# Half of the conditioning product moved from GpSimd and TensorE to row sums on VectorE

## The chip, the core and the metric

The kernel runs on one core of a Trainium2 chip. The core has a matrix engine (TensorE, PE in the profile; its loads of weights are shown as PEld), VectorE (DVE), ScalarE (ACT), GpSimd (POOL) and SyncE (SP), whose queue issues all the transfers of this kernel. Every engine runs its own queue in order, and engines wait for each other through semaphores. The metric is the device time of one execution in microseconds (us); lower is better.

## The reference

One decoder block over 1024 tokens of width 1024, float32. A conditioning vector `c` gives six vectors of 1024 that shift, scale and gate the two halves of the block:

```python
cond = jax.nn.silu(c)
mod = (cond @ w_ada[l] + b_ada[l]).astype(x.dtype)
sh_a, sc_a, gt_a, sh_m, sc_m, gt_m = [m[:, None, :] for m in jnp.split(mod, N_MOD, axis=-1)]

h = rms_norm(x, g_attn_pre[l]) * (1 + sc_a) + sh_a
proj = h @ w_in[l]
...
mixed = jnp.concatenate([rms_norm(oa, g_mix_a[l]), rms_norm(ob, g_mix_b[l])], axis=-1)
y = mixed @ w_out[l]
x = x + gt_a * rms_norm(y, g_attn_post[l])

h = rms_norm(x, g_mlp_pre[l]) * (1 + sc_m) + sh_m
y = jnp.square(jax.nn.relu(h @ w_up[l])) @ w_down[l]
x = x + gt_m * rms_norm(y, g_mlp_post[l])
```

`oa` and `ob` are the outputs of two attention mixers, a sliding window with sinks and a mixture of dilated windows. This study is about `sh_m` and `sc_m`, the shift and scale of the second modulation. They depend on `c` alone, and the first who needs them is the normalised input of the MLP.

## The kernel before

**Order of the work.** The program is written by a planner, the class `Sched` (lines 190 to 338). The kernel registers steps with an engine, a guessed duration, the steps they depend on and the buffers they take and give; `run` always emits the step that can start first by its own clock. What comes out is a fixed order for each engine. Buffers are counted in `Res` objects, such as `r_stg` for the ring of five staging tiles of 128x1024 (`stage`, line 471) and `r_wa` for the ring of first-modulation weights. So any edit of a duration, a buffer count or a step's start can reorder everything that the planner places after it.

**Stages.** In the start, until about 66 us, `x` is normalised and modulated, and the first of six projection units runs as its input comes in. The first modulation is made there on VectorE: `condb` (line 605) holds the vector `cond` spread over all 128 partitions; the host has laid out the first 2048 columns of `w_ada` by output channel (`w_mod`, line 117), a channel per partition, so that one multiply with a row sum (`ada_chunk`, line 687) gives 128 channels. `condb` lies in the pool `p0`, which is closed when the attention's pools open. Then units 1 to 5 of the projections (tile `pj`, lines 909 to 912) are interleaved on TensorE with the attention of the units already projected: scores (`s_ps`), softmax on VectorE, ScalarE and GpSimd (`p_sb`), transposes (`pt_ps`), the split of P into a high half on ScalarE and a low half on VectorE (`ph`, lines 1391 and 1495), and P times V (`o_ps`). The far branch of the dilated mixer has a chain of small VectorE steps (lines 1257 to 1291, tiles `z_far`, `y_far`, `a_far`) ahead of its scaling on GpSimd (line 1298). Projections end at about 356 us; the output projection (`y_ps`, lines 1815 to 1817) and the second normalisation follow, and from 473.7 us on the MLP (`mlp_ps`, lines 2250 to 2252) fills the rest.

**The rest of `mod`.** Columns 2048 to 6143 of `w_ada` are worked off in 32 pieces by `ada_piece` (line 1040), four pieces to a group of 512 columns. Groups 0 and 1 are the first gate, groups 2 and 3 `sh_m`, groups 4 and 5 `sc_m`, groups 6 and 7 the second gate. A piece loads 512 KB into a staging tile (`wa_st`, line 1046). Pieces 0 to 23 run on GpSimd: twice a product with a column of `cond` (line 1061; the first of a group writes the sum directly, line 1057) and an addition to `ada_acc` (line 1062). At a group's end TensorE sums `ada_acc` over the partitions. For a gate that is one matmul with a matrix of ones (line 1075); for shift and scale four matmuls of one column each turn the row into columns (line 1078), and VectorE adds the bias (lines 1109 to 1112). `feed_ada` (line 1115) lets piece i start when `st.d`, the count of projection units done, passes 1.0 + i * 4.1 / 24. Pieces 24 to 31 run on VectorE in the MLP (line 1059).

Of the kernel before, what the change touches and what calls it, by code (L numbers as in the profile page):

```python
# [10 lines left out]
F32 = mybir.dt.float32  # L11
# [4 lines left out]
ALU = mybir.AluOpType  # L16
# [3 lines left out]
P = 128  # L20
D = 1024
S = 1024
KC = D // P
# [54 lines left out]
def _columns():  # L78

    out = []  # L80
    for u in range(6):
        if u > 1:
            q = [512 + 128 * u + 64 * h for h in range(2)]
            k, v = [x + 512 for x in q], [x + 1024 for x in q]
            parts, rows = PARTS_B, ROWS_B
        else:
            g = u
            q, k, v = [256 * g + 64 * h for h in range(4)], [512 + 64 * g], [640 + 64 * g]
            parts, rows = PARTS_A, ROWS_A
        for c in range(3):  # L90
            got = [h + d for h in v for d in range(64)] if c == 2 else []
            got = [0] * (P - len(got)) + got
            for p, n, step, whose, row, ds in parts[c]:
                heads = q if whose == "q" else k
                got[p:p + n * step:step] = [h + rows[row + ds * r] for r in range(n // len(heads)) for h in heads]
            out += got
    return out


def _host(inputs):  # L100

    h = {n: np.ascontiguousarray(inputs[n]) for n in _INS if n != "w_mod"}
    c = np.zeros((P, CW), np.float32)
    c[:, CW_C:CW_C + KC] = inputs["c"][0].reshape(P, KC)
    c[:, CW_SINK:CW_SINK + 8] = inputs["sink_a"]
    b = inputs["b_ada"][0].reshape(48, P)
    c[:, CW_COL:CW_COL + 56] = np.concatenate(
        [inputs["g_attn_pre"][0].reshape(8, P), inputs["g_mlp_pre"][0].reshape(8, P), b[0:16], b[24:40],
         inputs["g_mix_a"][0].reshape(4, P), inputs["g_mix_b"][0].reshape(4, P)]).T
    w = h["w_in"][0][:, _columns()].reshape(2, 4, P, 18, P)  # L110
    w = np.ascontiguousarray(w.transpose(3, 0, 2, 1, 4)).reshape(36, P, 512)

    w[:6] = w[:6].reshape(3, 2, P, 4, P).transpose(2, 1, 3, 0, 4).reshape(P, 6, 512).transpose(1, 0, 2)
    h["w_in"] = w

    w = inputs["w_ada"][0][:, :2 * D].reshape(P, KC, 2, KC, P)
    h["w_mod"] = np.ascontiguousarray(w.transpose(3, 2, 4, 1, 0)).reshape(KC, 2, P, D)
    h["positions"] = np.ascontiguousarray(inputs["positions"][0].reshape(TB, P).T)
    _constants(c)
    h["consts"] = c  # L120
    return {n: h[n] for n in _INS + ["consts"]}


def _constants(c):
    c[:, CW_ID:CW_ID + P] = np.eye(P, dtype=np.float32)
    p = np.arange(P)[:, None]
    d = p + 384 - np.arange(512)[None, :]
    mult = ((d >= 0) & (d <= 128)).astype(int)
    mult += (d >= 0) & (d <= 512) & (d % 4 == 0)
    mult += (d >= 0) & (d % 16 == 0)  # L130
    neg = np.array([BIG, 0.0, -np.log(2.0), -np.log(3.0)], np.float32)
    c[:, CW_MB:CW_MB + 512] = neg[mult]
    d = p + P - np.arange(256)[None, :]
    c[:, CW_MN:CW_MN + P] = np.where(d <= 128, 0.0, BIG)[:, :P]
    c[:, CW_MN + P:CW_MN + 256] = c[:, CW_MB + 384:CW_MB + 512]
    c[:, CW_MF:CW_MF + P] = neg[(d <= 128).astype(int) + (d % 4 == 0)][:, :P]
    c[:, CW_MA:CW_MA + 256] = np.where((d >= 0) & (d <= 127), 0.0, BIG)
    m = np.arange(P)[None, :]
    c[:, CW_SW:CW_SW + P] = p % 32 == m // 4
    c[:, CW_SW + P:CW_SW + 2 * P] = p // 4 == m % 32  # L140
    c[:, CW_PK:CW_PK + 4] = p % 4 == m[:, :4]
    c[:, CW_PK + 4:CW_PK + 8] = p // 32 == m[:, :4]
    c[:, CW_SCL] = np.where(p[:, 0] % 2, 1.0, -0.125)
    c[:, CW_SCL + 1] = np.where(p[:, 0] < 64, -0.125, 1.0)
    c[:, CW_F:CW_F + 8] = np.array(INV_FREQ, np.float32)[None, :]
# [44 lines left out]
class Sched:  # L190
# [20 lines left out]
    def op(self, eng, dur, emit, deps=(), **kw):  # L211

        o = self.step(dur, emit, deps, **kw)
        o.alts = None
        if isinstance(eng, str):
            self.queue[eng].append(o)
        else:
            o.alts = dict(zip(eng, zip(dur, emit)))
            for e in eng:
                self.queue[e].append(o)  # L220
        return o.ev
# [131 lines left out]
def t_dv(n):  # L353
    return 0.066 + 0.00104 * n
# [19 lines left out]
def hybrid_block(ctx: ExitStack, tc: tile.TileContext, x, positions, w_mod, w_ada, b_ada, g_attn_post, w_in, w_out,  # L374
                 g_mlp_post, w_up, w_down, consts, out):
    nc = tc.nc
    ctx.enter_context(tc.manual_schedule())
    V, A, G, T = nc.vector, nc.scalar, nc.gpsimd, nc.tensor
    x, out = x[0], out[0]
    w_ada, w_out, w_up, w_down = w_ada[0], w_out[0], w_up[0], w_down[0]  # L380
    sc = Sched()
    op, pe_op = sc.op, sc.pe_op

    def pool(name, bufs=1, side="left", space=None, stack=ctx):
        kw = dict(name=name, bufs=bufs, reuse_waits="tile")
        if space is not None:
            kw["space"] = space
        else:
            kw["side"] = side
        return stack.enter_context(tc.tile_pool(**kw))  # L390
# [18 lines left out]
    r_pj, r_x, r_t, r_s, r_o, r_d = Res(2), Res(1), Res(2), Res(2), Res(1), Res(0)  # L409
    r_stg, r_w, r_wst, r_hl = Res(5), Res(WR), Res(WS), Res(0)  # L410
# [10 lines left out]
    cols = head[:, CW_COL - 8:CW_COL + 56]  # L421
# [6 lines left out]
    b1m = const.tile([P, KC], F32, name="b1m")  # L428
    g_a = const.tile([P, KC], F32, name="g_a")
    s_a = const.tile([P, KC], F32, name="s_a")  # L430
    g_m = const.tile([P, KC], F32, name="g_m")
    s_m = const.tile([P, KC], F32, name="s_m")
# [23 lines left out]
    p0 = pool("p0", 1, "right", stack=right0)  # L456
    pj = pool("pj", 2, space=PSUM)
    px = pool("px", 1, space=PSUM)
# [7 lines left out]
    st = Tok()  # L466
# [4 lines left out]
    def stage(name):  # L471
        return stgp.tile([P, 1024], F32, name=name, tag="stg")

    def load(emit, nbytes, deps=(), takes=(), prio=5, gives=(), after=None, n=1):
        return op("SP", nbytes / (345e3 if prio > -500 else 370e3), emit, deps, takes=takes, prio=prio, gives=gives, after=after, n=n)
# [16 lines left out]

    posi = p0.tile([P, TB], I32, name="posi")
    posf = p0.tile([P, TB], F32, name="posf")
    NWA, NH = 6, 3
    r_h = Res(NH)

    order0 = [("x", 0), ("x", 1), ("x", 2), ("x", 3), (0, 1), (0, 0), ("w", 0)]
# [99 lines left out]
    def f_cond():  # L598
# [3 lines left out]
        bc["diag"] = place0("diag")  # L602
        V.tensor_tensor(by_k(bc["diag"]), ident.unsqueeze(1).to_broadcast([P, KC, P]),
                        cond[:].unsqueeze(2).to_broadcast([P, KC, P]), ALU.mult)
    condb, bc = p0.tile([P, D], F32, name="condb"), {}
    e = e_cond = op("DVE", 0.52 + t_dv(D), f_cond, [e], takes=[(r_wa, 1)], prio=0)
    e_condb = []
    for n in range(2):
# [394 lines left out]
    def open_attention():  # L1003
        if any(x.t is None for x in e_tab[0] + e_tab[1] + list(e_hl.values())):
            return False
        nonlocal kring, qring, vfring, pprob, pth, opool, adp, mask_a, mask_b, mask_n, mask_f, swap, pick, e_mask
        right0.close()
        kw = dict(side="right", stack=right1)
        mkp = pool("mkp", 1, **kw)
        kring = pool("kring", NK, **kw)  # L1010
        qring = pool("qring", NQ, **kw)
        vfring = pool("vfring", NF, **kw)
        pprob = pool("pprob", NP, **kw)
        pth = pool("pth", NT, **kw)
        opool = pool("op", NO, **kw)
        adp = pool("adp", 1, **kw)
        r_k.give(sc.clk["PE"], NK)
        r_q.give(sc.clk["PE"], NQ)
        r_vf.give(sc.clk["PE"], NF)
        masks = mkp.tile([P, CW - CW_MB], F32, name="masks")  # L1020
        e_mask = load(lambda: nc.sync.dma_start(masks[:], consts[:, CW_MB:CW]), 724992, prio=-20)
        swap = [masks[:, 1152 + P * w:1152 + P * w + P] for w in range(2)]
        pick = [masks[:, 1408 + 4 * w:1412 + 4 * w] for w in range(2)]
        mask_b, mask_n = masks[:, 0:512], masks[:, 512:768]
        mask_f, mask_a = masks[:, 768:896], masks[:, 896:1152]
        sc.launch.append(feed_s)
        sc.launch.append(feed_ada)
        return True
# [5 lines left out]
    NADA = 24  # L1034
    ada = Tok()
    ada.i, ada.acc, ada.e, ada.raw, ada.gate = 0, None, Ev(0.0), {}, {}
    e_mod = {}
    r_adacc = Res(1)

    def ada_piece(i, eng, accp, psum, r_ps, r_acc=None):  # L1040
# [63 lines left out]
        else:  # L1104
# [7 lines left out]
                    V.tensor_tensor(g_m[:, k0:k0 + 4], g_m[:, k0:k0 + 4], cols[:, 16 + k0:20 + k0], ALU.mult)  # L1112
            e_mod[g] = op("DVE", 0.15, f_c, [ef], gives=[(r_ps, 1)], prio=4)

    def feed_ada():
        if st.d > 1.0 + ada.i * 4.1 / NADA and ada.i < NADA:
            ada_piece(ada.i, G, lambda: adp.tile([P, 512], F32, name="ada_acc", tag="ada_acc", bufs=1), lambda: px.tile([P, 512], F32, name="ada_ps", tag="x"), r_x)
            ada.i += 1
        return ada.i == NADA

# [1313 lines left out]
```

## Time and profile before

| what | value |
|---|---|
| median of 3 runs | 1099.63 us |
| runs | 1098.22, 1099.63, 2195.83 us |
| the profiled execution | 1098.02 us |
| its span, first to last instruction | 1096.2 us |
| granted TensorE clock, mean | 0.998 |
| TensorE busy | 1077.7 us |
| VectorE busy | 811.2 us |
| GpSimd busy | 285.0 us |

The shares of busy time are means over stages. What a part costs is read from the chain that ended last and from the waits, and a long busy time on an engine that nobody waits for costs nothing. In a row that lists an operation, `x16: 1271/1276/2321` is a count and the least, median and greatest duration in ns; in the rows by groups, `| 3.9, 242 |` is the busy time in us and the mean in ns. In a row of waits the numbers are the total in us, how often, and the longest. The third run, 2195.83 us, stands apart from the two others and is not used.

### The profile page before, as it was taken

The page shows a single profiled execution, that of the slowest core. Times are in us where ns is not written, and L with a number is a line of the kernel's source. Part 1 is how long each engine was busy: PE and PEld are TensorE (multiplying, and loading weights), DVE is VectorE, ACT ScalarE, POOL GpSimd, SP SyncE. Part 2 cuts the span into 40 slices and gives each one's busy share as a digit, 9 for nine tenths or more (in the row PEclk, how much of TensorE's full clock was granted, in tenths as well). Part 3 has the DMA queues.
Part 4 walks back from the last instruction along what each step waited for, and adds up shares of the span by engine and source line. Part 5 has one row for each costly group of instructions (what it writes and reads, how often), then busy time and mean ns, then how long its engine had stood idle before and what let it go on. Part 6 is the DMA issues. An engine that isn't in the chain of part 4 may idle for free.

```text
span 1096.2 us, 15266 instructions
## 1 busy us (share of the span) xinstructions
PE 1077.7 (98%) x5254; PEld 899.0 (82%) x5254; DVE 811.2 (74%) x1434; ACT 621.7 (57%) x1155; POOL 285.0 (26%) x378
## 2 busy tenths in 40 slices
PE   8999999999999999999999999999999999999996
PEld 6888888888888888888888888888888888888885
DVE  7968776766768687699796654897645995537998
ACT  6868876555556867686755244732245632337442
POOL 4649778596846531100000000000000000000002
PEclk9999999999999999999999999999999999999999
DMA  8565656454635457368711579231575043583104
GB/s 339 212 207 161 194 168 216 140 187 141 202 106 174 135 151 264 114 230 321 280 70 39 188 256 353 77 111 62 208 284 190 1 134 140 191 324 132 58 1 154
DMA packets 87230, 189.55 MB, mean 173 GB/s; under 512 B 8304, under 2 KB 24816, under 8 KB 87152
## 3 DMA queue, kind: packets, MB, share of 16 engines
q1 hardware_dynamic: 87152, 188.56, 49.6%
q8 instruction: 42, 0.69, 0.2%
q14 instruction: 36, 0.29, 0.1%
HBM read 139.25 MB, written 30.41 MB: 155 GB/s over the span
## 4 chain that ended last, share of the span: by engine, by line
PE 92%; DVE 4%; issue 1%; POOL 1%; ACT 1%; DMA 0%; DVEq 0%; POOLq 0%; SPq 0%
PE mlp_ps L2252 18%; PE mlp_ps L2250 18%; PE mlp_ps L2251 18%; PE pj L909 5%; PE pj L912 5%; PE pj L910 5%; PE y_ps L1815 3%; PE y_ps L1817 3%; PE y_ps L1816 3%; PE o_ps L1514 2%; PE s_ps L1323 1%; PE s_ps L1228 1%; PE o_ps L1415 1%; PE pt_ps L1380 1%; PE pt_ps L1479 1%
## 5 line engine op out<-in xcount | busy, mean ns | idle before, releaser
L2250 PE MATMUL mlp_ps<-hw 128*128 128x512 f32 x896 | 349.6, 390 | 0.0
L2252 PE MATMUL mlp_ps<-hw 128*128 128x512 f32 x896 | 348.6, 389 | 0.0
L2251 PE MATMUL mlp_ps<-hw 128*128 128x512 f32 x896 | 348.6, 389 | 0.0
L2251 PEld LDWEIGHTS mlp_ps<-hw 128*128 128x128 f32 x896 | 168.2, 188 | 35.3 <-issue 0.5
L2250 PEld LDWEIGHTS mlp_ps<-hw 128*128 128x128 f32 x896 | 168.2, 188 | 35.3 <-issue 0.5
L2252 PEld LDWEIGHTS mlp_ps<-hw 128*128 128x128 f32 x896 | 168.2, 188 | 34.9
L2017 DVE TENSOR_TENSOR hw<-w,hw 128x1024 fp32r<-128x1024 f32 x94 | 112.2, 1221 | 95.7 <-ACT hw L2010 93.0
L2010 ACT CAST hw<-w 128x1024 fp32r<-128x1024 f32 x94 | 95.7, 1050 | 129.8 <-PE mlp_ps L2252 94.5
L2350 POOL TENSOR_TENSOR st<-st,nhalf 128x1 f32<-128x1 f32 x8 | 7.8, 983 | 612.7 <-DVE st L2348 612.7
L909 PE MATMUL pj<-hw,w_hl 128*128 128x512 f32 x240 | 101.8, 424 | 0.0
L912 PE MATMUL pj<-hw,w_hl 128*128 128x512 f32 x240 | 94.5, 394 | 0.0
L910 PE MATMUL pj<-hw,w_hl 128*128 128x512 f32 x240 | 94.2, 392 | 0.0
L2010 ACT CAST hw<-u 128x1024 fp32r<-128x1024 f32 x48 | 48.7, 1053 | 64.5 <-PE mlp_ps L2252 64.5
L2017 DVE TENSOR_TENSOR hw<-u,hw 128x1024 fp32r<-128x1024 f32 x48 | 57.0, 1220 | 18.1 <-ACT hw L2010 18.1
L2308 DVE TENSOR_TENSOR yacc<-yacc,mlp_ps 128x512 f32<-128x512 f32 x96 | 62.2, 683 | 3.3 <-PE mlp_ps L2252 3.3
L1062 POOL TENSOR_TENSOR ada_acc<-ada_acc,wa_st 128x512 f32<-128x512 f32 x42 | 56.1, 1336 | 3.5
L912 PEld LDWEIGHTS pj<-hw,w_hl 128*128 128x128 f32 x240 | 45.0, 188 | 10.2
L1815 PE MATMUL y_ps<-hw,oh 128*128 128x512 f32 x128 | 51.6, 403 | 0.0
L1816 PE MATMUL y_ps<-hw,oh 128*128 128x512 f32 x128 | 50.0, 391 | 0.0
L909 PEld LDWEIGHTS pj<-hw,w_hl 128*128 128x128 f32 x240 | 45.4, 189 | 4.6
L910 PEld LDWEIGHTS pj<-hw,w_hl 128*128 128x128 f32 x240 | 45.5, 190 | 4.4
L2289 ACT ACTIVATE u<-u 128x512 f32<-128x512 f32 x48 | 29.0, 625 | 30.7 <-DVE u L2287 30.1
(259 smaller groups left out, 1988.3 us busy)
## 6 DMA issues: line engine op xcount, KB each, us to landing
hw<-s_dram SPq DMA_DIRECT2D x84, 512.0 KB, 4.1
wa_st<-in_w_ada SPq DMA_DIRECT2D x32, 512.0 KB, 4.5
w<-in_w_up SPq DMA_DIRECT2D x32, 512.0 KB, 4.7
w<-in_w_down SPq DMA_DIRECT2D x32, 512.0 KB, 6.8
s_dram<-hw SPq DMA_DIRECT2D x28, 512.0 KB, 3.2
qt<-hl SPq DMA_DIRECT2D x40, 256.0 KB, 2.5
w_st<-in_w_in SPq DMA_DIRECT2D x36, 256.0 KB, 3.0
x_sb<-in_x SPq DMA_DIRECT2D x16, 512.0 KB, 6.0
```

What stands on the lines that cost most here:

```text
L909: T.matmul(ps, w[:, 0, n], h[0], start=(k == 0), stop=False)
L910: T.matmul(ps, w[:, 1, n], h[0], start=False, stop=False)
L912: T.matmul(ps, w[:, 0, n], h[1], start=False, stop=(k == KC - 1))
L1062: G.tensor_tensor(ada.acc[:, :512], ada.acc[:, :512], wa[:, j], ALU.add)
L1815: T.matmul(ps[:], oh, wh[:, c0:c0 + 512], start=(k == 4 * m), stop=False)
L1816: T.matmul(ps[:], oh, wl[:, c0:c0 + 512], start=False, stop=False)
L2010: A.copy(out[j][0], flat(src[j]))
L2017: V.tensor_tensor(out[j][1], flat(src[j]), out[j][0].bitcast(F32), ALU.subtract)
L2250: T.matmul(ps[m][:], sh, mh, start=starts and k == 0, stop=False, **kw)
L2251: T.matmul(ps[m][:], sh, ml_, start=False, stop=False, **kw)
L2252: T.matmul(ps[m][:], sl, mh, start=False, stop=k == 3, **kw)
L2308: e = op("DVE", t_dv(512), lambda: V.tensor_tensor(y(), y(), ps[m][:], ALU.add), [e, ml.e_y[tb, n]], gives=gives, prio=1)
```

## The change

The eight GpSimd pieces of `sh_m` and the eight of `sc_m` (groups 2 to 5) are replaced by sixteen row sums on VectorE, in the way of the first modulation. The host lays out columns 3072 to 5119 of `w_ada` by output channel too and appends them to `w_mod`. A new function, `ada_rows`, loads 128 channels of shift or scale (512 KB) into a staging tile and makes one multiply with a row sum; bias, and 1 + for the scale, come in as the sum's start value, and for the scale one more small product with the norm's gain follows. The sums are chained: each waits for the one before it. TensorE has no part in it. `condb` has to live longer for that, so it moves from `p0` to a staging tile; one count is taken from `r_stg` until the last row sum has ended, which gives it back. The ring of first-modulation weights in `p0` gets a seventh tile (`NWA`). `feed_ada` starts piece i at `st.d` 2.0 + i * 3.2 / 24.

```diff
-    w = inputs["w_ada"][0][:, :2 * D].reshape(P, KC, 2, KC, P)
-    h["w_mod"] = np.ascontiguousarray(w.transpose(3, 2, 4, 1, 0)).reshape(KC, 2, P, D)
+    w = [inputs["w_ada"][0][:, c:c + 2 * D].reshape(P, KC, 2, KC, P) for c in (0, 3 * D)]
+    h["w_mod"] = np.concatenate([z.transpose(3, 2, 4, 1, 0).reshape(KC, 2, P, D) for z in w])
...
-    NWA, NH = 6, 3
+    NWA, NH = 7, 3
...
-    condb, bc = p0.tile([P, D], F32, name="condb"), {}
+    condb, bc = stage("condb"), {}
+    r_stg.free.pop()
...
+    def ada_rows(n):
+        which, k = divmod(n, KC)
+        dst, init = (g_m, b1m) if which else (s_m, cols[:, 40:48])
+        b = {}
+
+        def f_load():
+            b["w"] = stage("wa_st")
+            nc.sync.dma_start(b["w"][:], w_mod[KC + k, which])
+        el = load(f_load, 524288, takes=[(r_stg, 1)], prio=20)
+
+        def f_dot():
+            V.tensor_tensor_reduce(b["w"][:], b["w"][:], condb[:], 1.0, init[:, k:k + 1], ALU.mult, ALU.add,
+                                   dst[:, k:k + 1])
+            if which:
+                V.tensor_tensor(dst[:, k:k + 1], dst[:, k:k + 1], cols[:, 16 + k:17 + k], ALU.mult)
+
+        def after():
+            if n == 2 * KC - 1:
+                r_stg.give(sc.end)
+        ada.e2 = e_mod[2 + n // 4] = op("DVE", t_dv(D) + 0.22, f_dot, [el, ada.e2], gives=[(r_stg, 1)], prio=5,
+                                        after=after)
+    ada.e2 = Ev(0.0)
+
     def feed_ada():
-        if st.d > 1.0 + ada.i * 4.1 / NADA and ada.i < NADA:
-            ada_piece(ada.i, G, lambda: adp.tile([P, 512], F32, name="ada_acc", tag="ada_acc", bufs=1), lambda: px.tile([P, 512], F32, name="ada_ps", tag="x"), r_x)
+        if st.d > 2.0 + ada.i * 3.2 / NADA and ada.i < NADA:
+            if ada.i < 8:
+                ada_piece(ada.i, G, lambda: adp.tile([P, 512], F32, name="ada_acc", tag="ada_acc", bufs=1),
+                          lambda: px.tile([P, 512], F32, name="ada_ps", tag="x"), r_x)
+            else:
+                ada_rows(ada.i - 8)
             ada.i += 1
         return ada.i == NADA
```

**What moves in the order.** On TensorE, at the end of group 2, before. `q_far` are the far branch's queries, `pj` projection matmuls:

```order
L1228 MATMUL s_ps<-kt,q_far 128x128 x8
L1078 MATMUL ada_ps<-ones,ada_acc 128x1 x4
L909 MATMUL pj<-hw,w_hl 128x512
L910 MATMUL pj<-hw,w_hl 128x512
L912 MATMUL pj<-hw,w_hl 128x512
```

The same place in the changed kernel, whose lines are numbered one higher here and 28 higher behind the new function:

```order
L1256 MATMUL s_ps<-kt,q_far 128x128 x8
L910 MATMUL pj<-hw,w_hl 128x512
L911 MATMUL pj<-hw,w_hl 128x512
L913 MATMUL pj<-hw,w_hl 128x512
```

The four matmuls of one column are gone, and the projection follows the scores directly. Apart from the four such places TensorE has the same instructions; their order differs between the projection's second unit and the first matmuls of the MLP, and nowhere else.

On VectorE, the far branch's first pair of items before: the bias sum of `sh_m` (L1109), the sums that start the far chain (L1257, L1271, L1272) and the low halves of P (L1391):

```order
L1109 TENSOR_TENSOR s_m<-ada_ps,head 128x4
L1257 TENSOR_TENSOR z_far<-st_far,masks 128x32 x2
L1391 TENSOR_TENSOR ph<-pt_ps,ph 128x512
...
L1391 TENSOR_TENSOR ph<-pt_ps,ph 128x384
L1271 TENSOR_TENSOR y_far<-x_far,masks 128x32 x2
L1272 TENSOR_REDUCE st_far<-y_far 128x16
```

The same place in the changed kernel, with the first two row sums (L1127):

```order
L1127 ISA wa_st,s_m<-wa_st,condb,head 128x1024
...
L1419 TENSOR_TENSOR ph<-pt_ps,ph 128x512
L1419 TENSOR_TENSOR ph<-pt_ps,ph 128x384
L1285 TENSOR_TENSOR z_far<-st_far,masks 128x32 x2
...
L1271 ISA p_sb,st_far<-s_ps,masks 128x384
...
L1127 ISA wa_st,s_m<-wa_st,condb,head 128x1024
...
L1299 TENSOR_TENSOR y_far<-x_far,masks 128x32 x2
L1300 TENSOR_REDUCE st_far<-y_far 128x16
```

A row sum stands ahead of the two low halves of P, and another between the two parts of the far chain; both would hold up what is behind them if their loads were late.

On GpSimd, where the far branch's scalings stand (L1298 before), before:

```order
L1204 COPY q_far<-qt 128x1024
L800 TENSOR_TENSOR hl<-hl 128x512
L1061 TENSOR_SCALAR wa_st<-wa_st,cond 128x512
L1062 TENSOR_TENSOR ada_acc<-ada_acc,wa_st 128x512
L1061 TENSOR_SCALAR wa_st<-wa_st,cond 128x512
L1062 TENSOR_TENSOR ada_acc<-ada_acc,wa_st 128x512
L1298 TENSOR_SCALAR p_sb<-p_sb,a_far 128x256 x2
```

and in the changed kernel:

```order
L1232 COPY q_far<-qt 128x1024 x2
L801 TENSOR_TENSOR hl<-hl 128x512
L1326 TENSOR_SCALAR p_sb<-p_sb,a_far 128x256 x2
```

The products and sums of the accumulation no longer stand ahead of the scalings. The planner also gives GpSimd five more of the weight splits (L565) that VectorE had.

## The prediction

> **What bounds the kernel now.** I read the page from the top: busy shares, the granted clock in 40 slices, and the chain that ended last.
>
> ```profile
> PE 1077.7 (98%) x5254; PEld 899.0 (82%) x5254; DVE 811.2 (74%) x1434; ACT 621.7 (57%) x1155; POOL 285.0 (26%) x378
> ...
> PEclk9999999999999999999999999999999999999999
> ...
> PE 92%; DVE 4%; issue 1%; POOL 1%; ACT 1%; DMA 0%; DVEq 0%; POOLq 0%; SPq 0%
> ```
>
> TensorE (PE) is busy 98% of the span, 92% of the chain is its work, and its granted clock never moves. So a microsecond counts if it is PE work or a PE wait, and not otherwise. The PE waits, first over the whole run and then from 75 to 500 us:
>
> ```profile
> PE pxt L706 <- ACT x_sb L676: 3.9, 2, 2.8
> PE o_ps L1514 <- DVE ph L1495: 1.9, 2, 1.4
> PE acc L926 <- DVE nhalf L591: 1.5, 1, 1.5
> PE pm_o L1773 <- DVE ph L1495: 1.0, 1, 1.0
> PE ptab L753 <- issue: 0.4, 1, 0.4
> PE ada_ps L1078 <- POOL p_sb L1298: 0.2, 1, 0.2
> ```
>
> L706, L926 and L753 belong to the start. Later PE loses 1.9 + 1.0 + 0.2 = 3.1 us, nearly all behind VectorE (DVE). That is all the waiting there is to win, and a queue behind which more could be lost. The busy time by stretch (PE, PEld, DVE, ACT, POOL), with three short stretches for comparison:
>
> ```profile
> 66.00:190.00 124.00, 124.00 (x694) 104.62 (x693) 92.93 (x268) 92.89 (x255) 95.85 (x148) 1.00 0.64 197
> 190.00:310.00 120.00, 119.23 (x698) 103.06 (x697) 82.80 (x243) 66.21 (x175) 86.56 (x102) 1.00 0.48 155
> ...
> 100.00:125.00 25.00, 25.00 (x145) 21.24 (x144) 20.80 (x64) 21.58 (x64) 19.77 (x34) 1.00 0.53 160
> 375.00:400.00 25.00, 23.90 (x134) 19.88 (x134) 20.99 (x50) 15.52 (x31) 11.60 (x20) 1.00 0.24 79
> 475.00:500.00 25.00, 25.00 (x118) 20.83 (x116) 23.34 (x48) 21.16 (x42) 0.00 (x0) 1.00 0.62 234
> ```
>
> Where the new work goes (190 to 310 us) DVE is busy 82.8 of 120 us, 69%, GpSimd (POOL) 72%. DVE at 83% (100:125) and at 93% (475:500) stood beside a PE that lost nothing; at 84% (375:400) beside one that lost 1.1 us. DVE's share alone does not decide; what stands in its queue ahead of a PE input does.
>
> **The change, part by part.** The order on PE is the same up to about 70 us and again from about 487 us on, and its instructions are the same but for sixteen matmuls. So the start, the MLP and the tail stay, and everything below happens in between. The rows that date the projections (L909) and the MLP (L2250) in the old run:
>
> ```profile
> L909 PE MATMUL pj<-hw,w_hl x240: 387/397/500, 66.8 to 356.5; 128*128 128x512 f32 x120
> ...
> L2250 PE MATMUL mlp_ps<-hw x896: 389/389/798, 473.7 to 1086.0; 128*128 128x512 f32 x180
> ```
>
> *Removed from PE.* Four groups of tiny matmuls that turned the accumulated row into columns. Their line by groups, then their four pieces in the chain in order of time:
>
> ```profile
> L1078 PE MATMUL ada_ps<-ones,ada_acc 128*128 128x1 f32 x32 | 3.9, 242 | 0.2 <-POOL p_sb L1298 0.2
> ...
> 192.26 0.79 PE ada_ps L1078 x8
> ...
> 227.50 0.79 PE ada_ps L1078 x8
> ...
> 265.92 1.02 PE ada_ps L1078 x8
> ...
> 306.48 0.78 PE ada_ps L1078 x8
> ```
>
> The program has 16, the chip ran 32 passes. All four pieces lie on the chain: 0.79 + 0.79 + 1.02 + 0.78 = 3.4 us off the path. The neighbours on PE are projection matmuls that are ready, so I count all of it: -3.4.
>
> *Added to DVE.* Sixteen row sums of 128x1024. The first modulation does the same operation on the same shapes in the start, at L687 (rows for tiles condb and g_a):
>
> ```profile
> L687 DVE CUSTOM_DVE_ANT_0 wa<-wa,condb,bb x16: 1271/1276/2321, 12.6 to 53.1; 128x1024 f32<-128x1024 f32 x16
> ...
> L687 DVE DVE_READ_ACCUMULATOR2_ANT g_a<- x8: 76/78/80, 13.8 to 52.3; 128x1 f32 x8
> L691 DVE TENSOR_TENSOR g_a<-g_a,head x8: 159/160/247, 13.9 to 52.4; 128x1 f32<-128x1 f32 x8
> ```
>
> 16 x (1.276 + 0.078) + 8 x 0.160 = 23.0 us. Gone from DVE are the four small sums behind L1078 (1.0 us by the rows below), and the planner moves five weight splits (L565) to POOL, 5 x 0.79 = 4.0 us; other moves nearly cancel.
>
> ```profile
> L1109 DVE TENSOR_TENSOR s_m<-ada_ps,head x2: 156/157/158, 193.2 to 228.4; 128x4 f32<-128x4 f32 x2
> L1111 DVE TENSOR_TENSOR g_m<-ada_ps,b1m x2: 163/164/164, 267.0 to 307.3; 128x4 f32<-128x4 f32 x2
> L1112 DVE TENSOR_TENSOR g_m<-g_m,head x2: 166/180/195, 267.2 to 307.5; 128x4 f32<-128x4 f32 x2
> ...
> L565 DVE TENSOR_TENSOR w_hl<-w_st,w_hl 128x512 fp32r<-128x512 f32 x12 | 9.3, 790 | 1.7 <-ACT w_hl L560 1.4
> ```
>
> So DVE in the stretch 190:310 goes from 82.8 to about 101 of 120 us, 84%. The cover is its idle 37 us there; without any cover all sixteen would delay PE, +23. With perfect cover, and POOL's relief shortening the chains, PE's 3.1 us of waits could go as well. The rows above put PE's loss behind DVE at 2.9 us in this part of the run; at the 84% seen in 375:400 it was 1.1 us per 25 us, at 83% in 100:125 none. I take +1.0, near the lower end, because PE still has projection matmuls between the attention's until about 356 us, and keep -3.1 and +23 as bounds. What is late next, if a row delays anything, is the softmax maximum or the low half of P (ph) that is queued behind it, and then o_ps on PE.
>
> *Removed from POOL.* 28 products and 28 sums of the accumulation and four first products:
>
> ```profile
> L1062 POOL TENSOR_TENSOR ada_acc<-ada_acc,wa_st 128x512 f32<-128x512 f32 x42 | 56.1, 1336 | 3.5
> L1061 POOL TENSOR_SCALAR wa_st<-wa_st,cond 128x512 f32<-128x512 f32 x42 | 31.0, 738 | 19.1 <-DMA wa_st<-in_w_ada 19.1
> L1057 POOL TENSOR_SCALAR ada_acc<-wa_st,cond 128x512 f32<-128x512 f32 x6 | 4.2, 696 | 9.0 <-PE o_ps L1514 4.9 <-DMA wa_st<-in_w_ada 4.1
> ```
>
> 28 x (1.336 + 0.738) + 4 x 0.696 = 60.9 us. PE waited 0.2 us for POOL, so this is worth at most that directly; 0 in the sum.
>
> *Loads and staging.* Sixteen 512 KB loads replace sixteen of the same size on the same queue (SP), so their cost there stays. What moves is who waits: POOL before, DVE now. The pieces start later (in the order on the queues the first load stands some 35 projection groups further on), and while the spread condition holds its tile four staging tiles are left instead of five. In the start the DMA queue is in the same order with the same tiles in flight; the wait for a free buffer there falls on the weight stage (L551), which is unchanged: 0. In the middle a shorter ring makes SP wait sooner; no row prices that alone, and I put it between 0 and the longest wait for such a load, 9.6 us once:
>
> ```profile
> POOL wa_st L1061 <- DMA wa_st<-in_w_ada: 19.1, 7, 9.6
> ...
>   DMA wa_st<-in_w_ada: 26.0, 11
> ...
> DMA to landing us min/median/max: 3.5/4.5/9.1
> ```
>
> I take 0 for the middle, since the planner places the loads ahead by its own count of free tiles, and leave the upper end to the first rival.
>
> *Sum.* The profiled execution took 1098.02 us, 1096.2 of it span and 1.8 around it. 1098.0 - 3.4 + 1.0 = 1095.6. The shown runs that are comparable took 1098.22 and 1099.63, 0.2 and 1.6 above the profiled one; I add 0.4 and predict **1096 us**.
>
> **Rivals.** *A, slower than before: DVE stands behind late loads.* The place is a row sum whose load has not landed when DVE reaches it; DVE runs in order, so the far branch's softmax sums and the halves of P behind it wait too, and PE after them. For: POOL waited 26.0 us in 11 waits for these tiles (the row above). Two thirds of those pieces now wait on DVE: 26.0 x 16/24 = 17.3 us; if half of it reaches PE, 1098.0 - 3.4 + 8.7 = 1103.3, if all, 1111.9. Against: POOL was ahead of its loads because it had nothing else, and DVE takes the last eight such loads, in the MLP, with a longest wait of 2.3 us:
>
> ```profile
>   DVE ada_acc L1059: 2.3, 1
> ```
>
> It decides from 3.4 us of new PE waits on.
>
> *B, more gain: the waits go too.* With POOL 61 us lighter, the far chains end sooner and PE's 3.1 us vanish: 1098.0 - 3.4 - 3.1 = 1091.5. Against: those waits name DVE, which gets more work.
>
> *C, DVE and POOL block each other.* One of the sixteen sums at L687 took 2.32 us instead of 1.28. It began 0.06 us after a POOL sum of two tiles; the sum before it ran its 1.27 us beside POOL's table copies (start, duration):
>
> ```profile
> 45.18 2.53 POOL L747 COPY rows<-sinw 128x64 f32<-128x64 f32 x2
> 47.60 1.29 POOL L565 TENSOR_TENSOR w_hl<-w_st,w_hl 128x512 fp32r<-128x512 f32 x1
> ...
> 46.26 1.27 DVE L687 CUSTOM_DVE_ANT_0 wa<-wa,condb,bb 128x1024 f32<-128x1024 f32 x1
> ...
> 47.66 2.32 DVE L687 CUSTOM_DVE_ANT_0 wa<-wa,condb,bb 128x1024 f32<-128x1024 f32 x1
> ```
>
> If every new row lost 1.045 us (2321 less 1276 ns), DVE would hold 101 + 16.7 = 118 of 120 us; above the 93% that 475:500 shows without loss (112 us) PE would lose 6 us: 1098.0 - 3.4 + 6.1 = 1100.7. Against: one of sixteen lost it, and the change takes 28 of POOL's two-tile sums away. The Trainium skill (SBUF — State Buffer, Who interferes with whom) says that a VectorE instruction with two SBUF inputs and a GpSimd instruction that reads SBUF lock each other out for a whole instruction. The 2.32 us row agrees with that; the 1.27 us row beside the copies, which read SBUF too, does not show it.
>
> **How the numbers follow.** The forecast, 1092 to 1099, gets 0.66: the 3.4 us is certain and small. A gets 0.16, B 0.10, C 0.08. The range reaches into A and over B and C: **1091 to 1105 us**, leaving out A's upper part and a little of B. Two per cent is 22 us, about what a measurement of this kernel can tell from no change. Faster by that would need more than the 3.4 and 3.1 us there are: 0.01. Slower by that needs all sixteen rows and their loads on PE's path, the end of A: 0.04. Within 2%: 0.95. Whether it is faster at all is another matter; I hold that for 3 to 1.
>
> **What would show it.** In the profile after: no L1078 on PE, sixteen row sums of 1.28 us each near 190 to 310 us, DVE there at 98 to 104 us in 120, POOL down by about 50 us, and the MLP's first matmul some 2 to 3 us earlier than its 473.7 us. PE's waits after 75 us between 0 and 5 us confirm the +1.0. A shows as waits of DVE for wa_st above 5 us and of PE for ph or p_sb above 4 us; C as row sums with a median above 1.5 us. If the MLP begins earlier and the end does not move with it, the step that the MLP is a fixed block was wrong.

## The result: 1104.4 us, slower by 0.6%

| | before | after |
|---|---|---|
| median of the runs | 1098.1 us | 1104.4 us |
| ratio after to before, 95% interval | | 1.0058, 1.0046 to 1.0069 |
| profiled execution, span | 1096.2 us | 1102.4 us |
| first matmul of the MLP | 473.7 us | 479.9 us |
| MLP and tail on PE (first to last start of that row) | 612.3 us | 612.2 us |

The change costs 6.3 us by the medians. It is within 2%, and within the range of the prediction; but it is a loss, and a small gain was forecast. The whole loss lies ahead of the MLP, which begins 6.2 us later and then takes as long as before.

The page after, its busy shares and the chain that ended last:

```profile
PE 1077.4 (98%) x5222; PEld 895.8 (81%) x5222; DVE 827.7 (75%) x1462; ACT 621.1 (56%) x1146; POOL 238.2 (22%) x332
...
PE 86%; DVE 5%; DMA 2%; issue 2%; ACT 2%; POOL 1%; SPq 0%; DVEq 0%; POOLq 0%; ACTq 0%
```

POOL lost 46.8 us and PE its 32 passes of L1078. But PE has 86% of the chain instead of 92%, and DMA stands there with 2%: work that lay beside PE now lies in its path. The waits of PE from 75 to 500 us (what waited, for what, us in total, times, longest):

```profile
PE pv L866 <- ACT vt L860: 2.2, 1, 2.2
PE pv L866 <- DVE ot L1467: 1.8, 1, 1.8
PE s_ps L1256 <- DMA o_dram<-ot: 1.4, 1, 1.4
PE pt_ps L1507 <- POOL p_sb L1326: 1.0, 1, 1.0
PE pj L910 <- DVE hl L812: 0.9, 1, 0.9
PE o_ps L1542 <- DVE ph L1523: 0.9, 1, 0.9
PE s_ps L1256 <- DVE st_far L1271: 0.8, 2, 0.4
PE y_ps L1845 <- DVE ol L1786: 0.7, 1, 0.7
PE x_far L1292 <- DVE z_far L1285: 0.6, 1, 0.6
PE pt_ps L1507 <- DVE y_far L1299: 0.5, 1, 0.5
PE pj L910 <- ACT vt L860: 0.3, 1, 0.3
PE px L1913 <- ACT xn L1901: 0.2, 1, 0.2
```

These add up to 11.3 us, against 3.1 before: 8.2 new. No one wait is the culprit. From 75 us to the first matmul of the MLP, first before, then after (the stretch, its length, then busy time of PE, PEld, DVE, ACT, POOL):

```profile
75.00:473.70 398.70, 395.36 (x2215) 337.43 (x2215) 294.23 (x792) 268.84 (x651) 239.92 (x320) 1.00 0.53 171
75.00:479.90 404.90, 393.63 (x2182) 332.72 (x2181) 309.81 (x819) 268.62 (x644) 198.14 (x275) 1.00 0.51 168
```

PE's idle time grew from 3.3 to 11.3 us, by 7.9, and its busy time fell by 1.7; together that is the 6.2 us. The busy time fell by less than the 3.4 us taken from PE, so other work of PE took longer in these records; why is left open. By stretch, in the kernel after:

```profile
66.00:190.00 124.00, 120.52 (x671) 100.74 (x670) 90.75 (x258) 88.69 (x240) 74.99 (x134) 1.00 0.53 167
190.00:310.00 120.00, 115.46 (x663) 98.72 (x662) 95.52 (x266) 67.13 (x174) 66.27 (x74) 1.00 0.54 185
```

The first stretch is the surprise. In it, from 66 to 190 us, PE loses 3.5 us, where it lost nothing before, and the first row sum starts only at 197.7 us. So part of the loss is not the row sums at all. What happened at 175 to 189 us, first on SP's queue, then on GpSimd, then on ScalarE (start, duration, in brackets the idle time before):

```profile
173.25 1.90 SPq L1488 DMA_DIRECT2D o_dram<-ot  x2
178.08 0.38 SPq L1047 DMA_DIRECT2D wa_st<-in_w_ada  x1
...
180.77 0.55 SPq L551 DMA_DIRECT2D w_st<-in_w_in  x1
```
```profile
182.55 1.28 POOL L1063 TENSOR_TENSOR ada_acc<-ada_acc,wa_st 128x512 f32<-128x512 f32 x1
```
```profile
178.46 0.59 ACT L1415 CAST ph<-pt_ps 128x512 fp32r<-128x512 f32 x1 [1.20 <-PE pt_ps L1408]
183.87 0.69 ACT L809 ACTIVATE hl<-pj,head 128x512 fp32r<-128x512 f32 x1 [4.82 <-DMA w_st<-in_w_in]
...
188.65 0.60 ACT L860 COPY vt<-pj 128x512 f32<-128x512 f32 x1
```

L809 takes a finished projection (pj) out of PSUM, the memory in which TensorE's results stand until another engine takes them, into a tile hl, and it stood 4.8 us. The profile names a weight load, which L809 does not read. It writes hl, and hl comes from the staging ring (`b["f"] = stage("hl")`), the same ring as wa_st. GpSimd's last read of a wa_st tile ends at 182.55 + 1.28 = 183.83 us, and L809 starts at 183.87. The trace's semaphores agree: the last one that L809 waits for is raised by GpSimd alone, at 183.84 us. So the projection waited for a staging tile that a condition load held. Until it was out, its PSUM bank was not free, L860 and the values behind it came late, and PE stood three times between 184 and 192 us: `pj` 0.9, `pv` 2.2, `s_ps` 1.4.

The second part is the row sums. Their rows by groups (busy time, mean ns; idle time before them), and the small multiply behind the second eight (ns min/median/max):

```profile
L1127 DVE CUSTOM_DVE_ANT_0 wa_st<-wa_st,condb,head 128x1024 f32<-128x1024 f32 x8 | 12.3, 1533 | 2.2 <-POOL p_sb L1326 1.7 <-DMA wa_st<-in_w_mod 0.5
...
L1127 DVE CUSTOM_DVE_ANT_0 wa_st<-wa_st,condb,b1m 128x1024 f32<-128x1024 f32 x8 | 10.8, 1350 | 3.8 <-DMA wa_st<-in_w_mod 3.8
```
```profile
L1130 DVE TENSOR_TENSOR g_m<-g_m,head x8: 158/160/1820, 255.4 to 312.2; 128x1 f32<-128x1 f32 x8
```

They took 12.3 + 10.8 = 23.1 us (20.4 foreseen). The eight multiplies took 4.0 us (1.3 foreseen), most of it in two of them, 1.12 us at 291.19 and 1.82 at 306.78. DVE waited 0.5 + 3.8 us for the sums' loads. One place shows what that does, at 305 to 309 us (POOL's cast began at 305.60 and took 2.98):

```profile
305.36 1.38 DVE L1127 CUSTOM_DVE_ANT_0 wa_st<-wa_st,condb,b1m 128x1024 f32<-128x1024 f32 x1 [1.15 <-DMA wa_st<-in_w_mod]
...
306.78 1.82 DVE L1130 TENSOR_TENSOR g_m<-g_m,head 128x1 f32<-128x1 f32 x1
308.52 0.41 DVE L1467 TENSOR_TENSOR ot<-o_ps,otmp 64x256 f32<-64x256 f32 x1
...
308.99 0.66 PE L866 MATMUL pv<-head,vt 128*128 128x128 f32 x4 [1.80 <-DVE ot L1467]
```

A late load (1.15), a row sum (1.38) and a multiply of one column that took 1.82 us instead of 0.16 stand in front of an output (ot) that PE needs.

### The profile page after: what moved, and what is told of

It reads as the page before. It is cut to its first block, busy times and chain, and to the rows that moved or that the text cites. A ratio compares the mean times of both kernels' runs of the same rounds, so it can differ in the third digit from the quotient of the medians.

```text
span 1102.4 us, 15190 instructions
## 1 busy us (share of the span) xinstructions
PE 1077.4 (98%) x5222; PEld 895.8 (81%) x5222; DVE 827.7 (75%) x1462; ACT 621.1 (56%) x1146; POOL 238.2 (22%) x332
## 4 chain that ended last, share of the span: by engine, by line
PE 86%; DVE 5%; DMA 2%; issue 2%; ACT 2%; POOL 1%; SPq 0%; DVEq 0%; POOLq 0%; ACTq 0%
PE mlp_ps L2279 18%; PE mlp_ps L2278 17%; PE mlp_ps L2280 17%; PE pj L910 4%; PE pj L913 4%; PE pj L911 4%; PE y_ps L1843 2%; PE y_ps L1845 2%; PE y_ps L1844 2%; DMA wa_st<-in_w_mod 2%; PE o_ps L1542 1%; PE s_ps L1351 1%; PE o_ps L1443 1%; PE pt_ps L1408 1%; PE acc L910 1%
## 5 line engine op out<-in xcount | busy, mean ns | idle before, releaser
L1326 POOL TENSOR_SCALAR p_sb<-p_sb,a_far 128x128 f32<-128x128 f32 (+3 forms) x60 | 33.3, 577 | 44.3 <-DVE a_far L1319 32.7
```

The source lines that it names most:

```text
L1326: return lambda: eng.tensor_scalar(rec.pw[w][j], rec.pw[w][j], b["a"][:, w, j:j + 1], 1.0, ALU.mult, ALU.mult)
```

## The experiments

Two theories at the outset. **R**: the ring of four tiles instead of five costs the time. **D**: the row sums in VectorE's queue do. All ratios are to the kernel before, run on the same chip, with the 95% interval. Before took 1097.5 to 1098.8 us there, so medians of different rows can be compared to about 1 us.

| run | what it is | median us | ratio to before |
|---|---|---|---|
| e1_ring4 | before, four tiles | 1104.9 | 1.0063 (1.0049 to 1.0078) |
| e2_short | after, sums of 64 columns | 1100.7 | 1.0028 (1.0017 to 1.0038) |
| e3_ring5 | after, five tiles | 1099.7 | 1.0013 (1.0003 to 1.0022) |
| e4_nofin | before, no L1078 | 1092.4 | 0.9949 (0.9935 to 0.9963) |
| e5_dates | before, the new dates | 1096.4 | 0.9980 (0.9969 to 0.9991) |
| e6_r5short | after, five tiles, 64 columns | 1097.0 | 0.9985 (0.9973 to 0.9996) |
| e7_fold | after, one multiply | 1102.6 | 1.0041 (1.0027 to 1.0055) |
| e8_reload | after, five tiles until the sums, one multiply | 1099.3 | 1.0007 (0.9994 to 1.0021) |
| e9_ring4_held | e1, loads held back | 1097.0 | 0.9989 (0.9980 to 0.9998) |
| e10_held | after, loads held back | 1101.6 | 1.0033 (1.0019 to 1.0047) |
| e11_reload_held | e8, loads held back | 1101.7 | 1.0035 (1.0021 to 1.0050) |
| e12_late_sums | after, sums later | 1101.1 | 1.0029 (1.0019 to 1.0040) |
| e13_reload_late | e8, sums later | 1093.8 | 0.9957 (0.9943 to 0.9971) |
| e14_held_late | e10, sums later, one multiply | 1092.9 | 0.9955 (0.9938 to 0.9972) |
| e15_held_late_8 | e10, sums later | 1093.8 | 0.9961 (0.9948 to 0.9975) |
| e16_gpsimd_held | before, dates, held, later | 1096.0 | 0.9981 (0.9972 to 0.9989) |

**One part alone: the ring.**

```diff
--- before
-    NWA, NH = 6, 3
+    NWA, NH = 7, 3
-    condb, bc = p0.tile([P, D], F32, name="condb"), {}
+    condb, bc = stage("condb"), {}
+    r_stg.free.pop()
...
+               after=(lambda: r_stg.give(sc.end)) if i == NADA - 1 else None)
```

> The kernel before, with one part of the change alone: the spread condition sits in a staging tile until the last piece of the condition product, so four staging tiles are left instead of five; the product stays on GpSimd and TensorE, at the old dates. Theory R (the shorter ring makes SP wait for a free tile, the weights come late and PE stands; that is most of the loss at 184 to 192 us): 3 to 6 us slower than before, 1101 to 1104. Theory D (the row sums in VectorE's queue cost the time): within 1 us of before, 1097 to 1099.

Measured 1104.9, 6.1 us above before: the ring alone costs as much as the whole change. The first two rows of PE's waits after 75 us:

```profile
PE pj L910 <- DVE hl L795: 3.5, 1, 3.5
PE o_ps L1516 <- DVE ph L1497: 2.3, 2, 1.3
```

The 3.5 us stand at 107 us: again a projection that PE cannot begin, because earlier ones still stand in PSUM. L795 is the last step on DVE that takes the newest of them out. The one ahead of it was finished at 92.3 us, and ScalarE came to it 15.6 us later:

```profile
107.94 0.59 ACT L809 ACTIVATE hl<-pj 64x512 fp32r<-64x512 f32 x1
```

In before the same step (L808) starts at 95.36 us, 1.0 us behind its projection. ScalarE did not stand idle ahead of 107.94: here the order has the step late, which fits a planner that counts no free tile, while at 183 us of the kernel after the engine itself waited for one.

**Undoing one part, and taking the sums' time away.** e2 cuts the operands of the row sum to `[:, :64]`, nothing else. e3 puts the condition back and lets the sums read another tile:

```diff
--- after
-    condb, bc = stage("condb"), {}
-    r_stg.free.pop()
+    condb, bc = p0.tile([P, D], F32, name="condb"), {}
...
-            V.tensor_tensor_reduce(b["w"][:], b["w"][:], condb[:], 1.0, init[:, k:k + 1], ALU.mult, ALU.add,
+            V.tensor_tensor_reduce(b["w"][:], b["w"][:], tabs[0][:], 1.0, init[:, k:k + 1], ALU.mult, ALU.add,
```

> The kernel after, in the same order of instructions, with each of the sixteen row sums cut to the first 64 of its 1024 columns (the rest of the product is left out); loads and staging stay. It takes about 16 x 1.15 = 18 us of VectorE's work away. Theory D: PE no longer waits behind the row sums at 223, 275 and 307 us, 4 to 5 us faster than after, about 1100. Theory R: no more than 1 to 2 us faster than after, 1102.5 to 1103.5, and the waits at 184 to 192 us stay.

> The kernel after with five staging tiles: the spread condition stays where it was before, and the row sums multiply by the first rotary table (128x1024 in the same type) instead, so the second modulation's values are not the condition's. The sixteen row sums keep their number, shape and length. Theory R: 4 to 5 us faster than after, 1099 to 1100.5, and the waits at 184 to 192 us are gone. Theory D: within 1.5 us of after, 1103 to 1105.

> The kernel after with five staging tiles (row sums against the rotary table, as in e3_ring5) and each row sum cut to 64 of 1024 columns, the rest left out. e3_ring5 took 1099.7 and the kernel before without L1078 took 1092.4, so 7.3 us lie between. Theory D (VectorE's time in the row sums is those 7 us): 1092.5 to 1095. If the loads, the dates and the new order are part of it: 1096 to 1099.

e3 (1099.7) took 4.7 us from after, as R said, and its list has none of the three waits at 184 to 192 us; e2 (1100.7) took 3.7, nearly what D said, and keeps them. Both are at work. e6, with both, came to 1097.0, still 4.6 above e4's 1092.4 (4.0 by the ratios): the time inside the sums is not all of it.

**What L1078 was worth.** The matmuls are left out, and the small sums read the accumulator:

```diff
--- before
-            else:
-                for k in range(4):
-                    T.matmul(b[0][:, k:k + 1], ada.acc[:, k * P:(k + 1) * P], ones[:, 0:1], start=True, stop=True)
```

> The kernel before without the four groups of 128x1 matmuls at L1078 (the sums over partitions are left out; VectorE's small sums read the accumulator itself). If all four pieces of the chain leave the path, as the prediction counted, 3.4 us faster than before: 1094.5 to 1095. If PE only finds other idle time in their place, within 1 us of before: 1097 to 1099.

By the ratio 0.9949 it is worth 5.6 us, 4.1 to 7.1, not 3.4. The profiled MLP began at 468.5, 5.2 us earlier than in before. From 66 us to there PE's busy time was 4.3 us less (400.09 against 404.36) and its waits after 75 us were 0.9 us shorter. The term was right in sign and too small.

**The dates alone** (`2.0 + ada.i * 3.2 / NADA` in the kernel before):

> The kernel before with the change's dates for the 24 pieces alone (2.0 + i*3.2/24 instead of 1.0 + i*4.1/24); five staging tiles, the product on GpSimd and TensorE. If the dates and the new order that they bring cost nothing by themselves: 1097.5 to 1100. If a good part of the loss is another order of the same work: 1101 or more.

1096.4: a little faster than before. The new order that the dates bring does not cost; and an order changed by nothing but dates moves the time by 2 us, so differences of that size between two orders are given no cause below.

**One multiply instead of eight.**

```diff
--- after
-            if which:
-                V.tensor_tensor(dst[:, k:k + 1], dst[:, k:k + 1], cols[:, 16 + k:17 + k], ALU.mult)
+            if which and k == KC - 1:
+                V.tensor_tensor(dst[:], dst[:], cols[:, 16:24], ALU.mult)
```

> The kernel after with the eight multiplies of 128x1 behind the second eight row sums folded into one of 128x8 behind the last. One of the eight took 1.82 us instead of 0.16 in the profile after, at 306.8 us beside a GpSimd cast of 128x1024, and PE stood 1.8 us behind it. If such small operations cost by standing beside GpSimd: 1.5 to 3 us faster than after, 1101.5 to 1103. If another operation only takes the hit: within 1 us of after, 1103.5 to 1105.

1102.6: 1.8 us off, but its interval overlaps that of after. The waits for ot (1.8 us) and for ph (0.9) are gone from its list, those at 184 to 192 us stay. What the fold is worth here is not settled.

**Five tiles until the sums begin.** One row of the condition goes to DRAM in the start and is loaded before the first sum:

```diff
--- after
+    e_cd = load(lambda: nc.sync.dma_start(cond_d[0:1, :], condb[0:1, :]), 4096, list(e_condb), prio=-4)
...
+            nc.sync.dma_start(ada.cb[:], cond_d[0:1, :].to_broadcast([P, D]))
+        if n == 0:
+            ada.e_cb = load(f_cl, 524288, [e_cd], takes=[(r_stg, 1)], prio=19)
```

> The kernel after with five staging tiles until the row sums begin: the spread condition stays in the start's own tile, one row of it goes to DRAM (4 KB), and it is loaded into a staging tile only before the first row sum and given back after the last; the eight multiplies are folded into one. Computes the whole reference. Theory R (the short ring costs most at 100 to 192 us, where projections are evacuated into these tiles): 1098.5 to 1101. If the short ring costs as much during the row sums: 1103 to 1105.

1099.3, as R said: the short ring is dear before the sums begin, not during them. It has the fold of e7 in it too, which may be up to 2 us of the 5.1.

**Is it the projections that lack a tile?** In e9 and e10 a load of the product may take a tile only when three are free, and gives two back at once:

```diff
--- after, the rows (the pieces on GpSimd likewise, there and in e9)
-        el = load(f_load, 524288, takes=[(r_stg, 1)], prio=20)
+        el = load(f_load, 524288, takes=[(r_stg, 3)], prio=20, after=lambda: r_stg.give(sc.clk["SP"], 2))
```

> e1_ring4 (the kernel before with four staging tiles), with one rule added: a load of the condition product (the pieces on GpSimd) is issued only when three of the four tiles are free, so that two stay for the projections, whose rotated and split halves are written into tiles of the same ring. Theory H (the loss of the short ring is projections that find no tile to be evacuated into, and PE that waits for their PSUM bank): most of e1_ring4's 6 us come back, 1098 to 1100.5. If the short ring costs because the loads themselves come late: as slow as e1_ring4 or slower, 1104 and more.

> The kernel after with the same rule alone: pieces and rows are loaded only when three tiles of the ring are free. Theory H: about what five tiles gave (e3_ring5 1099.7), 1098.5 to 1101. Against H: within 1 us of after, 1103.5 to 1105.5, or slower because the row sums now wait for later loads.

> e8_reload with the same rule, the version of the change that the runs so far point to (five tiles until the row sums, loads held back, one multiply). Computes the whole reference. Theory H: faster than e8_reload's 1099.3, 1095 to 1098, so level with the kernel before or a little faster. If the row sums' place in VectorE's queue is what is left: as e8_reload, 1098.5 to 1100.5.

e9 settles the ring: still four tiles, and 1097.0 instead of 1104.9, 7.9 us less, well above the 2 us of another order. Loads that go out later cost nothing there; what cost was the tile taken from the projections. From 66 to 190 us, e1 first, then e9, where PE loses 0.5 us instead of 4.6; and PE's waits after 75 us in e9:

```profile
66.00:190.00 124.00, 119.45 (x652) 99.52 (x651) 91.60 (x255) 89.44 (x244) 89.06 (x141) 0.99 0.62 190
66.00:190.00 124.00, 123.49 (x689) 104.15 (x688) 93.69 (x269) 93.84 (x254) 83.17 (x136) 1.00 0.60 187
```
```profile
PE o_ps L1517 <- DVE ph L1498: 1.4, 1, 1.4
PE pm_o L1776 <- DVE ph L1498: 1.0, 1, 1.0
PE pt_ps L1383 <- POOL p_sb L1358: 0.3, 1, 0.3
```

For the row sums the same rule was a miss: e10 gained 2.9 us instead of the 3.4 to 5.9 expected, and e11 lost 2.4 against e8. With the ring cured, something of the sums was left. In e10 it grew with the later loads: DVE's waits for them were 8.2 us, against 4.2 in after. In e11 they were not longer (6.4 us, against 6.8 in e8), so what e11 lost stays open. DVE's waits in e10 for these tiles, and one place:

```profile
DVE wa_st L1128 <- DMA wa_st<-in_w_mod: 8.2, 6, 2.8
```
```profile
296.62 0.56 DVE L1420 TENSOR_TENSOR ph<-pt_ps,ph 128x384 fp32r<-128x384 f32 x1 [0.20 <-ACT ph L1416]
299.73 1.61 DVE L1128 CUSTOM_DVE_ANT_0 wa_st<-wa_st,condb,b1m 128x1024 f32<-128x1024 f32 x1 [2.55 <-DMA wa_st<-in_w_mod]
...
301.39 1.83 DVE L1131 TENSOR_TENSOR g_m<-g_m,head 128x1 f32<-128x1 f32 x1
303.14 0.41 DVE L1468 TENSOR_TENSOR ot<-o_ps,otmp 64x256 f32<-64x256 f32 x1
```

DVE does nothing for PE from 297.2 to 303.1 us: 2.55 us before a load that has not landed, then the sum, then the multiply; PE waited 2.8 us for that ot. The planner counts at least 1.1 + 1.5 + 0.8 = 3.4 us from a load's issue to its landing. For the sixteen loads of the row sums in e10 it was

```profile
DMA to landing us min/median/max: 3.7/4.7/6.0
```

so a sum can stand in DVE's order ahead of the time at which its data land (in after it was 3.5, 3.8 and 6.1 us).

**Sums behind the real landing.** The planner is told that the row sum's load lands 2.5 us later; nothing waits longer on the chip for that, only the order is another:

```diff
--- after
+        def late():
+            el.t += 2.5
-        el = load(f_load, 524288, takes=[(r_stg, 1)], prio=20)
+        el = load(f_load, 524288, takes=[(r_stg, 1)], prio=20, after=late)
```

> The kernel after, with each row sum planned 2.5 us later behind its load than the planner counts, so that the order on VectorE has the sum behind the load's real landing; nothing else is changed (four tiles, no loads held back). Theory A of the prediction (VectorE stands in front of late loads and the softmax work is queued behind): VectorE's waits for these tiles fall from 4.2 us to under 1, and the time by 1.5 to 3 us, 1101.5 to 1103. If the sums' own time and place is what costs: within 1 us of after, 1103.5 to 1105; if each tile held 2.5 us longer starves the ring more: above 1105.

> e8_reload with the same later sums; computes the whole reference. Theory A: its 6.8 us of VectorE's waits go and the time falls to 1096 to 1098, level with before. If not the waits but the sums' time and the order cost what is left: 1098.5 to 1100.5.

> e10_held (loads only with three tiles free) with the same later sums and the eight multiplies folded into one; computes the whole reference, with the four tiles of the change. Theory A: VectorE's 8.2 us of waits and PE's 2.8 us behind them go, 1096.5 to 1099. If not: 1099.5 to 1102.

All three gained: 3.3 us from after, 5.6 from e8, 8.7 from e10, the last two more than expected. DVE's waits for these loads fell to 0.2 us in e12 and 0.6 in e13, and to none in e14. e12 keeps the waits at 182 to 192 us (its list still has `pv` behind vt at 2.2), as it must with the ring as it was. PE's waits after 75 us in e14, and its middle stretch:

```profile
PE pm_o L1805 <- DVE ph L1527: 1.0, 1, 1.0
PE o_ps L1447 <- DVE den L1221: 0.6, 1, 0.6
PE pj L910 <- ACT vt L860: 0.3, 1, 0.3
PE pm_o L1805 <- ACT hl L809: 0.3, 1, 0.3
```
```profile
190.00:310.00 120.00, 120.00 (x692) 103.62 (x691) 96.05 (x273) 69.07 (x184) 70.00 (x77) 1.00 0.55 187
```

The same row of e10:

```profile
190.00:310.00 120.00, 115.88 (x657) 99.46 (x657) 96.20 (x264) 64.53 (x168) 64.50 (x76) 0.99 0.55 188
```

DVE is as busy there in both, 96 of 120 us; PE loses 4.1 us in e10 and nothing in e14.

**Which part of e14, and are the sums worth anything?** e15 is e14 with the eight multiplies back. e16 has held loads, dates and later steps on the kernel before, without row sums.

> e14_held_late with the eight multiplies of 128x1 left as the change has them, so that it differs from e10_held by the later sums alone; computes the whole reference. If the late loads carry the 8.7 us between e10_held (1101.6) and e14_held_late (1092.9): 1092.5 to 1095. If the folded multiply carries a good part: 1096 to 1099.

> The kernel before with everything that helped except the row sums: the change's dates, loads of the product only with three of its five tiles free, and its GpSimd steps planned 2.5 us later behind their loads; the product stays on GpSimd and TensorE. If the row sums themselves are worth something once nothing stands late in front of them (PE rid of L1078: 5 us by e4_nofin, less what VectorE's fuller queue costs): 1096 to 1098, above e14_held_late by 3 to 5 us. If the gain of e14_held_late is all held loads and dates: 1092 to 1094.5.

e15 took 1093.8: the later sums alone made 7.7 of the 8.7 us, and the fold makes no difference that can be told. e16 took 1096.0, about what the dates alone gave (e5, 1096.4), so held loads and later steps bring nothing more where GpSimd does the work. Against e15 and e14 that leaves 2 to 3 us for the row sums in themselves, under the 5.6 that L1078 had cost; with 2 us between two orders and intervals that just overlap, this is not shown to be more than nothing. e14, 0.45% faster than before (0.28 to 0.62%), keeps the change's four tiles and computes the whole reference; e13 and e15 cannot be told from it.

## Why the prediction was wrong, step by step

- **PE bounds, MLP and tail are a block.** Held: 98% busy, 612.3 against 612.2 us.
- **-3.4 for L1078.** Right in sign, too small: 5.6 us, 4.1 to 7.1 (e4_nofin). The four pieces of the chain were not all: PE's busy time fell by 4.3 us and its waits by 0.9.
- **DVE's new work, 23.0 us in all.** Too small: the sums took 23.1 instead of 20.4 us and the eight multiplies 4.0 instead of 1.3. DVE was at 95.5 of 120 us, not 101. But DVE's share decided nothing: at 96 of 120 us PE lost nothing in e14. "What stands in its queue ahead of a PE input does" was the right sentence, and the sum did not follow it.
- **"I take 0 for the middle", loads and staging. This step failed, and it is the larger of the two.** It asked only when a load would find a free tile and who waits for the load (at most 9.6 us, once). The ring also holds the projections' results. A tile less is a projection left in PSUM, and the next one on PE waits for the bank. Alone it costs 6.1 us (e1_ring4), and five tiles gave 4.7 us back in the change itself (e3_ring5); the loads' lateness had no part in it (e9_ring4_held).
- **+1.0 for new waits, near the lower end. Failed too:** 8.2 us of new waits. Besides the ring it is the first rival, A: DVE in front of loads that have not landed. In the change as it stands it is worth 3.3 us (e12_late_sums). Its price, 8.7 us "if half of it reaches PE", is near what the sums' lateness cost in e10 (7.7 us, against e15), but that is luck: of the 26.0 us that it was worked out from, POOL waited 23.2 (19.1 and 4.1) and DVE the rest, and the half was a guess. The mark set for A, over 5 us of DVE waits for wa_st and over 4 us behind ph or p_sb, was not reached in after (4.2, and 0.9 + 1.0): it was too narrow, since PE also waited for ot and y_far, and with the sums cut short (e2_short) ot fell from 1.8 to 0.8 us while y_far and ph went.
- **C, DVE and POOL block each other.** The effect is there: the sums' mean was 1.444 us ((12.3 + 10.8) / 16) instead of 1.276. It did not decide: in e13 the second eight have a median of 1.77 us, over the 1.5 that was to show C, and it is 3.8 us faster than before; in e12 the sums took 27.5 us in all, and it is faster than after. One reading in C was wrong. The 1.27 us row beside the table copies was said not to show the block, but there it was GpSimd that stood: the copy took 1.33 us, where most of the same copies at 123 to 128 us took 0.30.

```profile
46.37 1.33 POOL L747 COPY rows<-sinw 128x64 f32<-128x64 f32 x1
```

- **POOL's relief worth 0.** Not tried by itself. POOL fell by 46.8 us, about the 50 foreseen.
- **The range and the odds.** 1104.4 lies within 1091 to 1105, at its upper end, because the range reached into A; the cost that was largest, projections left in PSUM, was in none of the cases, so that is luck in part. The 3 to 1 for faster was wrong. The cases were weighed by who waits for a load, not by who else lives in the ring.

What stays open: the parts do not add up singly (held loads alone gave 2.9 us, later sums alone 3.3, both 10.6). Each of them also changes the order of everything behind it, and up to 2 us of any difference may come from that alone.

## What to carry to other kernels

Before a buffer is taken from a ring, list everything that lives in it: if results of the bounding engine do, a buffer less is that engine's output with no place to go, and loads are the ones to hold back. Work that moves onto an in-order engine goes behind the measured landing of its data (here 4.7 us at the median in e10 against 3.4 planned), since everything queued behind it waits as well. The share of busy time of that engine says little: VectorE at 80% (96 of 120 us) stood beside a TensorE that lost 4.1 us in one order and nothing in another.

## What the runs showed of the hardware

A VectorE multiply of a single column, 128x1, normally 0.16 us, took 1.82 us in after and 1.83 in e10_held, both times beside GpSimd's cast of q_far. In after the cast was

```profile
305.60 2.98 POOL L1232 CAST q_far<-qt 128x1024 fp32r<-128x1024 f32 x1
```

306.78 + 1.82 = 308.60 on DVE and 305.60 + 2.98 = 308.58 on POOL: it ended with the cast. It goes the other way too. At 289.72 us a GpSimd sum (L565) of 1.29 us took 2.57, while a row sum that began 0.16 us after it kept its 1.27; the multiply behind that, at 291.19 us, took 1.12 us and ended with the GpSimd sum (292.31 against 292.29). The table copy of the kernel before, shown above, ended 0.16 us after the row sum beside it (47.70 against 47.54). So where these meet, one stands until the other's instruction is over. The Trainium skill (SBUF — State Buffer, Who interferes with whom) states such a lock for a VectorE instruction with two SBUF inputs beside a GpSimd instruction that reads SBUF; these rows agree, and the prediction had given it less than they show. What it costs depends on what is queued behind. In e14 the folded multiply met such a cast as well:

```profile
304.86 2.02 POOL L1236 CAST q_far<-qt 128x1024 fp32r<-128x1024 f32 x1 [4.17 <-PE s_ps L1260]
304.90 2.00 DVE L1134 TENSOR_TENSOR g_m<-g_m,head 128x8 f32<-128x8 f32 x1
```

PE has no wait from 300 to 312 us there, and one multiply or eight made no difference that can be told (e14 against e15).
